# Rope tables in one pass, norms and index scores in PSUM, and the edge of the mixer masks: one change to a two-block model kernel

## The chip, the cores and the metric

The kernel runs as one program on one core of a Trainium2 chip. The metric is the device time of one execution in microseconds (us), taken as the median of several runs. The engines are TensorE (PE, with PEld for its weight loads), VectorE (DVE), ScalarE (ACT), GpSimd (POOL) and SyncE (SP), which here only issues DMAs. Each engine works through its own queue in order.

## What is computed

Two model blocks run one after the other over the same 256 tokens of width 1024, in 32-bit floating point, batch 1. The first block has four layers; layers 0 and 3 use attention over keys chosen by an index score, layers 1 and 2 other attention. Each layer also attends to 256 memory rows, which are normed once, and ends in a gated feed-forward part. Cut to what the change touches:

```python
cos, sin = rope_tables(positions)                  # theta 500000, 8 frequencies
mem_n = layer_norm(mem, mem_ln_g, mem_ln_b)
for i in range(4):
    if i % 3 == 0:
        q, k, v, qi, wi, ki, qm = split_cols(x @ w_in_a[j], ...)
        ki = apply_rope(layer_norm(ki, idx_kn_g[j], idx_kn_b[j]), cos, sin)
        wi = wi * (IDX_HEADS * IDX_DIM) ** -0.5
        # in dsa_attention, for each query block:
        dots = jnp.einsum('bqhd,bsd->bqhs', qi, k_idx)             # 8 heads of 64
        score = jnp.einsum('bqhs,bqh->bqs', jax.nn.relu(dots), wi)
        _, sel = lax.top_k(score, 64)                              # causal; attention to sel alone
    ...
    x = layer_norm(ALPHA * x + mixed, ...); x = layer_norm(ALPHA * x + swiglu(x, ...), ...)
```

The second block has two layers. The first mixes with a recurrence (its decay and causal masks are the "mixer masks") and a gating part, the second with latent attention that has a rope of its own (theta 10000, 16 frequencies, positions 0 to 255). Both attend to a second memory of 256 rows and end in a mixture of 32 experts.

## The kernel before, in words

Tokens lie in two row tiles of 128 (`NT = 2`). A projection (`proj`) streams its weights by SP's DMA in pieces of 1 MB into one of three `raw` buffers; `unit` (L274) splits each 128x512 piece into a high part, written by ACT (L294, `wh`), and a low part, the rest, written by POOL (L296, `wl`), or by DVE in a few stages. `mac` (L304) then issues three products for each piece and row tile (L311 to L313). 12 pairs of weight buffers lie between ACT and POOL on one side and PE on the other. PSUM has three rings: `mm` (4 banks, projection results), `tp` (2 banks, transposes), `at` (2 banks, attention scores). `w2` is a ring of four 128x512 tiles in SBUF for passing values, `sm` a ring of eight small ones.

The program is written in the order of the layers, but each engine's queue is put in order by a planner, which plays the program through with costs of its own and gives an engine the earliest written of the instructions that are ready. An instruction with no late inputs is therefore issued early wherever its engine has a gap in the plan. `issue_after(ins)` adds an edge for order alone to what a block issues: instructions of the block on the engine of `ins` are queued behind `ins`; instructions on other engines get no edge.

What the change and the steps of the prediction touch:

- `setup` (L403) and `setup2` (L914) make the rope tables of the two blocks, for each row tile by itself: an angle, then `rotation` (L423), which calls `sin_reduced` (L449) for cosine and sine (range reduction on DVE, L453 to L464, and a Sin on ACT, L465) and copies each result with a sign (L427, DVE).
- `rotate` (L467) applies a table to a head: three DVE operations (L472 to L474).
- `mem_setup` (L666) norms the two memory tiles on DVE (`norm_affine`: L160 and L166 for halves of 512 columns) and transposes them on PE (L142), with a split by ACT (L150) and DVE (L151).
- `sink_idx` (L739) takes the columns of index weights, index key and memory query out of PSUM. The key norm is L752 to L754 into an SBUF tile `c`, then the rope, then a second copy of the key beside the first (L757), then transposes (L494).
- `topk` (L838) makes the scores: for each group of heads PE writes 512 columns of an `at` bank (L848), ACT copies them through Relu to an SBUF tile (L850), and DVE adds them up, one operation for each head (L853, L855). With row tile 0 there are two groups of four heads with 128 columns each, with row tile 1 four groups of two heads with 256 columns. It is a generator, advanced between the projections of layers 0 and 3.
- `attn_mem` (L635) takes the maximum of memory scores (L655), then Exp on ACT (L659).
- `proj_post` (L199) ends a layer half: the product, a norm of each row tile on DVE (`norm(0)`, `norm(1)`) and the transposes of each (`turn(0)`, `turn(1)`, on PE). It keeps `self.normed`, the last DVE instruction of `norm(1)`. At the join of the two blocks, `mem2_setup` (L976) transposes the second memory and `mixer_masks` (L941, 25 DVE operations and 6 iotas on POOL) makes the masks, both in a block behind `self.normed`. The mask tiles belong to a pool that reuses the SBUF of the first block's pool.

Of the kernel before, what the change touches and what calls it, by code (L numbers as in the profile page):

```python
# [20 lines left out]
NT = 2  # L21
# [13 lines left out]
class K:  # L35
# [163 lines left out]
    def proj_post(self, x, w, kdim, xs, alpha, g, b, xT=None, between=None, **kw):  # L199


        last = []

        def norm(t, ps):
            with self.tc.issue_after(last[-1].ins) if last and not between else nullcontext():
                st = self.ln_stats()
                for i in range(2):
                    self.ln_half(xs[t], ps, alpha, i, st)
                last.append(self.ln_end(xs[t], ps, st, g, b, between=between and (lambda rs: between(t, rs))))

        def turn(t):
            return self.transposed(xs[t], t, xT) if xT else None

        ps = self.proj_full(x, w, kdim, after=lambda ps: norm(0, ps), before=lambda: turn(0), **kw)
        norm(1, ps)
        self.normed = last[-1]
        turn(1)

# [173 lines left out]
D_FF = 2816  # L392
INV_A = [float(np.float32(500000.0) ** np.float32(-np.float32(i) / np.float32(8))) for i in range(8)]
SCALE = 0.125
LAG1 = 8
# [5 lines left out]
class First(K):  # L401

    def setup(self, A):  # L403
        nc = self.nc
        self.A = A
        c = self.const
        self.cmask2 = self.s1.tile([128, 256], F32, name="cmask2")
        nc.vector.tensor_scalar(self.cmask2, self.cmask, NEG, None, op0=OP.add)

        self.cs = c.tile([128, NT, 2, 2, 8], F32, name="cs")  # L410
        inv = c.tile([128, 8], F32, name="inv")
        for i in range(8):
            nc.vector.memset(inv[:, i:i + 1], INV_A[i])
        for t in range(NT):
            pi = self.sm(1, I32)
            nc.gpsimd.dma_start(out=pi, in_=A["positions"][0, t * 128:(t + 1) * 128].rearrange("(p o) -> p o", o=1))
            pf = self.sm(1)
            nc.vector.tensor_copy(out=pf, in_=pi)
            ang = self.sm(8)
            nc.vector.tensor_scalar(ang, inv, pf, None, op0=OP.mult)  # L420
            self.rotation(self.cs[:, t], ang)

    def rotation(self, cs, ang):  # L423

        for j, off in ((0, math.pi / 2), (1, 0.0)):
            self.sin_reduced(cs[:, j, 1, :], ang, off)
            self.nc.vector.tensor_scalar(cs[:, j, 0, :], cs[:, j, 1, :], -1.0 if j else 1.0, None, op0=OP.mult)  # L427

# [19 lines left out]

    def sin_reduced(self, out, ang, off):  # L449
        nc = self.nc  # L450
        n = ang.shape[-1]
        k = self.sm(n)
        nc.vector.tensor_scalar(k, ang, 1.0 / (2 * math.pi), off / (2 * math.pi), op0=OP.mult, op1=OP.add)  # L453
        nc.vector.tensor_scalar(k, k, 12582912.0, 12582912.0, op0=OP.add, op1=OP.subtract)
        r = self.sm(n)
        c1 = 6.28125
# [7 lines left out]
        nc.vector.tensor_scalar(r, r, math.pi, -math.pi, op0=OP.min, op1=OP.max)  # L464
        nc.scalar.activation(out=out, in_=r, func=AF.Sin)  # L465

    def rotate(self, out, h, cs, b):  # L467

        nc = self.nc
        sh = list(h.shape)  # L470
        bc = lambda a: a[:, None].to_broadcast(sh)
        nc.vector.tensor_tensor(b, h[:, :, ::-1, :], bc(cs[:, 1]), op=OP.mult)  # L472
        nc.vector.tensor_tensor(h, h, bc(cs[:, 0]), op=OP.mult)
        nc.vector.tensor_tensor(out, h, b, op=OP.add)  # L474

    def rope(self, out, v, t):
# [3 lines left out]
        b = self.s1.tile([128, 8, 2, 8], F32, tag="rope", name="ropeb", bufs=4)[:, :nh]  # L480
        self.rotate(two(out), two(v), self.cs[:, t], b)

# [183 lines left out]
    def mem_setup(self, ms):  # L666
# [4 lines left out]
        for t, m in enumerate(ms):  # L671
            mv = self.stats(m, D)
            self.norm_affine(m, m, mv, g, b, 1e-5)
            self.transposed(m, t, self.memT)
# [19 lines left out]
    def layer_body(self, i, xs, xT):  # L694
# [40 lines left out]
        if kind == 0:  # L735
# [3 lines left out]
            def sink_idx(chunk, ps):  # L739
                for t in range(NT):  # L740
# [9 lines left out]
                    self.rsqrt(rs, mvv[:, 1:2], 1e-5)  # L750
                    kn = c[:, 0:64]
                    nc.vector.tensor_scalar(kn, kv, mvv[:, 0:1], rs, op0=OP.subtract, op1=OP.mult)  # L752
                    nc.vector.tensor_tensor(kn, kn, kng, op=OP.mult)
                    nc.vector.tensor_tensor(kn, kn, knb, op=OP.add)  # L754
                    self.evac(c[:, 128:384], ps[t][:, 72:328], 256)
                    self.rope(kn[:, None, :], kn[:, None, :], t)
                    nc.vector.tensor_copy(out=c[:, 64:128], in_=kn)  # L757
                    self.qk_transposed(smT, c, t, [0, 128, 256], 4)
# [79 lines left out]
    def topk(self, t, smT, wi, amask):  # L838
# [5 lines left out]
        for hs in [range(a + par, a + 2 * per, 2) for a in range(0, 8, 2 * per) for par in range(2)]:  # L844
            p = self.at((128, per, W))
            for j, h in enumerate(hs):
                r = slice(64 * (h % 2), 64 * (h % 2) + 64)
                nc.tensor.matmul(p[:, j, :], smT[r, h // 2, t * 128:(t + 1) * 128], smT[r, 4, 0:W], start=True, stop=True)  # L848
            rl = self.w2((128, per, W))
            nc.scalar.activation(out=rl, in_=p, func=AF.Relu)  # L850
            for j, h in enumerate(hs):
                if h == 0:
                    nc.vector.tensor_scalar(acc, rl[:, j, :], wi[:, 0:1], 0.0, op0=OP.mult, op1=OP.add)  # L853
                else:
                    nc.vector.scalar_tensor_tensor(acc, rl[:, j, :], wi[:, h:h + 1], acc, op0=OP.mult, op1=OP.add)  # L855
            yield
# [35 lines left out]
DN = 4.0 ** 0.25  # L892
INV_M = [float(np.float32(10000.0) ** np.float32(-np.float32(i) / np.float32(16))) for i in range(16)]
DECAY = -0.5 * math.exp(-0.5)
# [17 lines left out]
class Second(First):  # L912

    def setup2(self, A):  # L914
# [13 lines left out]
        nc.vector.memset(self.ones, 1.0)  # L928

        self.cs2 = c.tile([128, NT, 2, 2, 16], F32, name="cs2")  # L930
        inv = c.tile([128, 16], F32, name="inv2")
        for i in range(16):
            nc.vector.memset(inv[:, i:i + 1], INV_M[i])
        for t in range(NT):
            pos = self.sm(1)
            nc.gpsimd.iota(pos, pattern=[[1, 1]], base=128 * t, channel_multiplier=1, allow_small_or_imprecise_dtypes=True)
            ang = self.sm(16)
            nc.vector.tensor_scalar(ang, inv, pos, None, op0=OP.mult)
            self.rotation(self.cs2[:, t], ang)

# [35 lines left out]
    def mem2_setup(self):  # L976
        nc = self.nc
        self.mem2T = self.pair(self.xa, "mem")
        for t in range(2):
            m = self.raw()[:, 0:D]  # L980
            nc.sync.dma_start(out=m, in_=self.A2["mem"][0, t * 128:(t + 1) * 128, :])
            with self.tc.issue_after(self.normed.ins):
                self.transposed(m, t, self.mem2T, self.at)
# [26 lines left out]
    def mixer_ab(self, xT, side):  # L1010
        nc = self.nc
        A = self.A2
        cols, half = self.params_T()
        with self.tc.issue_after(self.normed.ins):
            self.mixer_masks(self.s2)
# [444 lines left out]
    def rope2(self, out, v, t):  # L1460
        two = lambda x: x.rearrange("p h (a d) -> p h a d", a=2)
        b = self.s2.tile([128, 4, 2, 16], F32, tag="rope", name="ropeb", bufs=4)[:, :v.shape[1]]
        self.rotate(two(out), two(v), self.cs2[:, t], b)

# [545 lines left out]
```

## Time and profile before

| what | value |
|---|---|
| time, median of 3 runs | 2957.38 us (2955.36 to 2957.61) |
| the profiled execution's own time | 2956.99 us |
| its span, first to last instruction | 2954.8 us |
| mean granted TensorE clock | 0.951 of full |
| PE busy | 2623.8 us (89%), 13571 products |
| DVE busy | 1418.1 us (48%), 3091 instructions |
| ACT busy | 897.8 us (30%), 1760 instructions |
| POOL busy | 1024.6 us (35%), 809 instructions |
| moved by DMA | 697.41 MB, mean 236 GB/s |

A row of a timeline is: start in us from the span's start, duration in us, engine, line, operation, tile written and tiles read (names without buffer numbers), shapes, and the count where neighbouring instructions of one kind are merged (the duration is then that of all). In brackets stands how long the engine stood idle before, and what it was waiting for. A row of windows has the stretch, its length, the busy time of PE, PEld, DVE, ACT and POOL with their counts, the granted clock of PE (1.00 is 2.4 GHz, 0.50 is 1.2 GHz), the busy share of DMA and GB/s. A duration holds time in which the instruction had started but could not go on.

### The profile page before, as it was taken

How to read it: one execution, taken by the hardware profiler on the slowest of the kernel's cores; microseconds unless marked ns; L12 is line 12 of the kernel's file. 1: busy time of each engine (PE TensorE's matmuls, PEld its weight loads, DVE VectorE, ACT ScalarE, POOL GpSimd, SP SyncE). 2: the span in 40 equal slices, each digit the busy share in tenths (PEclk: the TensorE clock that was granted, in tenths of full speed). 3: DMA queues.
4: the chain of work that ended last, by engine and by line, in shares of the span. 5: the costliest groups of instructions: out<-in, count | busy, mean ns of one | idle time of the engine just before them, and what ended most of it. 6: DMA issues, size and time to landing. Idle time of an engine off the chain costs nothing. (4 is left out here: it accounts for less than half of the span.)

```text
span 2954.8 us, 36636 instructions
## 1 busy us (share of the span) xinstructions
PE 2623.8 (89%) x13571; PEld 1833.6 (62%) x13571; DVE 1418.1 (48%) x3091; ACT 897.8 (30%) x1760; POOL 1024.6 (35%) x809
## 2 busy tenths in 40 slices
PE   6899999999999998999899989888787899877885
PEld 5678876888778876887788867322232776322331
DVE  8867645765466577675874665110011755100112
ACT  3455443554455445454422132000000642000000
POOL 6445582656645573555444341000000531000000
PEclk8899998999999999999999999999999999999989
DMA  6335552555445543554423346999999547999997
GB/s 199 121 116 188 182 199 86 188 182 191 136 145 187 184 161 115 165 177 162 150 86 103 111 164 234 399 422 421 421 421 401 177 179 280 397 421 421 421 422 307
DMA packets 201220, 697.41 MB, mean 236 GB/s; under 512 B 12874, under 2 KB 43712, under 8 KB 153920
## 3 DMA queue, kind: packets, MB, share of 16 engines
q1 hardware_dynamic: 195264, 676.57, 61.4%
q0 software_dynamic: 5760, 18.32, 1.8%
q8 instruction: 111, 1.82, 0.2%
q14 instruction: 85, 0.70, 0.1%
HBM read 693.80 MB, written 1.05 MB: 235 GB/s over the span
## 5 line engine op out<-in xcount | busy, mean ns | idle before, releaser
L296 POOL TENSOR_TENSOR wl<-raw,wh 128x512 fp32r<-128x512 f32 (+1 forms) x520 | 724.1, 1418 | 604.4 <-ACT wh L294 588.7
L294 ACT ACTIVATE wh<-raw 128x512 fp32r<-128x512 f32 (+1 forms) x776 | 479.7, 628 | 326.5 <-PE mm L312 183.5
L311 PE MATMUL mm<-wh,xh 128*128 128x512 f32 (+2 forms) x1152 | 454.7, 397 | 12.9 <-DVE w L92 8.9
L296 POOL TENSOR_TENSOR wq<-raw,wq 128x512 fp32r<-128x512 f32 (+2 forms) x160 | 206.5, 1315 | 701.8 <-DMA raw<-in_mla_w_in_dram 459.7
L312 PE MATMUL mm<-wh,xl 128*128 128x512 f32 (+2 forms) x1152 | 449.6, 391 | 0.0
L313 PE MATMUL mm<-wl,xh 128*128 128x512 f32 (+2 forms) x1152 | 448.7, 391 | 0.0
L296 DVE TENSOR_TENSOR wl<-raw,wh 128x512 fp32r<-128x512 f32 x256 | 358.9, 1426 | 143.6 <-PE mm L312 90.1
L311 PEld LDWEIGHTS mm<-wh,xh 128*128 128x128 f32 x1152 | 221.2, 192 | 59.8 <-ACT cs L465 9.3
L1877 ACT ACTIVATE w<-at 128x512 f32<-128x512 f32 x16 | 9.6, 597 | 817.9 <-PE at L1869 817.9
L312 PEld LDWEIGHTS mm<-wh,xl 128*128 128x128 f32 x1152 | 221.7, 192 | 43.3 <-issue 1.0
L313 PEld LDWEIGHTS mm<-wl,xh 128*128 128x128 f32 x1152 | 220.4, 191 | 44.2 <-issue 0.7
L294 ACT ACTIVATE wq<-raw 128x512 fp32r<-128x512 f32 (+2 forms) x196 | 109.1, 611 | 247.3 <-issue 117.5
L1665 POOL TENSOR_TENSOR x<-x,gb 128x512 f32<-128x512 f32 x2 | 3.5, 1726 | 465.3 <-DVE x L1664 465.3
L1869 PE MATMUL at<-mraw,xg 128*32 128x512 f32 x432 | 120.2, 678 | 31.6 <-DMA mraw<-in_moe_w_up_dram 22.7
L1869 PE MATMUL at<-wq,xg 128*32 128x512 f32 x464 | 124.2, 662 | 26.3 <-DMA wq<-in_moe_w_up_dram 17.9
L1852 PEld LDWEIGHTS tp<-oh,x 128*128 128x128 f32 x512 | 125.0, 334 | 32.9 <-issue 21.1
L1852 PE MATMUL tp<-oh,x 128*128 128x128 f32 x512 | 130.6, 411 | 14.2 <-PEq L1671 10.1
L1869 PE MATMUL at<-xl,xg 128*32 128x512 f32 x240 | 129.0, 672 | 12.8 <-DMA xl<-in_moe_w_gate_dram 8.5
L1878 DVE SCALAR_TENSOR_TENSOR w<-w,at 128x512 f32<-128x512 f32 x16 | 11.0, 687 | 259.4 <-ACT w L1877 259.4
L311 PE MATMUL mm<-wh,big 128*128 128x512 f32 x352 | 134.4, 391 | 0.0
L312 PE MATMUL mm<-wh,big 128*128 128x512 f32 x352 | 133.2, 389 | 0.0
L1879 DVE SCALAR_TENSOR_TENSOR w<-w,at 128x512 f32<-128x512 f32 x16 | 11.0, 688 | 250.4 <-PE at L1869 250.4
(586 smaller groups left out, 5092.2 us busy)
## 6 DMA issues: line engine op xcount, KB each, us to landing
raw<-in_w_gate_up_dram SPq DMA_DIRECT2D x80, 1024.0 KB, 5.2
raw<-in_w_down_dram SPq DMA_DIRECT2D x44, 1024.0 KB, 4.9
mraw<-in_moe_w_down_dram SPq DMA_DIRECT2D x31, 1024.0 KB, 19.8
wq<-in_moe_w_up_dram SPq DMA_DIRECT2D x30, 1024.0 KB, 19.8
mraw<-in_moe_w_gate_dram SPq DMA_DIRECT2D x28, 1024.0 KB, 19.8
wq<-in_moe_w_gate_dram SPq DMA_DIRECT2D x28, 1024.0 KB, 19.8
raw<-in_moe_w_up_dram SPq DMA_DIRECT2D x26, 1024.0 KB, 19.8
mraw<-in_moe_w_up_dram SPq DMA_DIRECT2D x26, 1024.0 KB, 19.8
```

Of the source, the lines that this page charges most:

```text
L294: nc.scalar.activation(out=hi, in_=src, func=AF.Copy)
L296: (nc.vector if on_dve else nc.gpsimd).tensor_tensor(lo, src, hi.bitcast(F32), op=OP.subtract)
L311: nc.tensor.matmul(p, xh, hi[:, a:b], start=first, stop=False)
L312: nc.tensor.matmul(p, xl, hi[:, a:b], start=False, stop=False)
L313: nc.tensor.matmul(p, xh, lo[:, a:b], start=False, stop=last)
L1665: (nc.vector if t else nc.gpsimd).tensor_tensor(xs[t][:, s], xs[t][:, s], b[:, s], op=OP.add)
L1852: nc.tensor.matmul(p[:, j, :], xs[t].rearrange("p (q k) -> p k q", k=8)[:, kc, :], O[t], start=(t == 0), stop=(t == 1))
L1869: nc.tensor.matmul(p[ss, :], x[:, ss], got[u][m * i + j], start=first, stop=last, tile_position=(0, s0))
L1877: nc.scalar.activation(out=h, in_=gu[0], func=AF.Tanh, scale=0.5)
L1878: nc.vector.scalar_tensor_tensor(h, h, 1.0, gu[0], op0=OP.add, op1=OP.mult)
L1879: nc.vector.scalar_tensor_tensor(h, h, 0.5, gu[1], op0=OP.mult, op1=OP.mult)
```

## The change

One table tile now holds both blocks' frequencies (8 and 16) for both row tiles, made in `setup`, ahead of the first weights in the written order: one range reduction over 48 columns for the cosine and one for the sine, in `w2` tiles, and the signed copies are Sins of their own. `setup2` makes no table. In `sink_idx` the key is normed and scaled in place in its PSUM bank; its columns 16 to 64 and its second copy are written by ACT, the rope reads the bank and writes `c`. In `topk` Relu is done in place in the `at` bank and DVE reads the bank. The memory norm is one ACT operation for each half into an `at` bank, a DVE product in the bank and a DVE sum into SBUF. `self.turned` takes the place of `self.normed`: it is what `turn(1)` returns (`transposed` returns its last PE transpose), or the norm's last instruction where nothing is turned.

```diff
         ps = self.proj_full(x, w, kdim, after=lambda ps: norm(0, ps), before=lambda: turn(0), **kw)
         norm(1, ps)
-        self.normed = last[-1]
-        turn(1)
+        self.turned = turn(1) or last[-1]
...
-        self.cs = c.tile([128, NT, 2, 2, 8], F32, name="cs")
-        inv = c.tile([128, 8], F32, name="inv")
-        for i in range(8):
-            nc.vector.memset(inv[:, i:i + 1], INV_A[i])
+        nf = len(INV_A + INV_M)
+        self.cs = c.tile([128, 2, 2, NT, nf], F32, name="cs")
+        inv = c.tile([128, nf], F32, name="inv")
+        for i, v in enumerate(INV_A + INV_M):
+            nc.vector.memset(inv[:, i:i + 1], v)
+        ang = self.w2()[:, :NT * nf].rearrange("p (t n) -> p t n", t=NT)
+        n1 = len(INV_A)
         for t in range(NT):
             pi = self.sm(1, I32)
             nc.gpsimd.dma_start(out=pi, in_=A["positions"][0, t * 128:(t + 1) * 128].rearrange("(p o) -> p o", o=1))
             pf = self.sm(1)
             nc.vector.tensor_copy(out=pf, in_=pi)
-            ang = self.sm(8)
-            nc.vector.tensor_scalar(ang, inv, pf, None, op0=OP.mult)
-            self.rotation(self.cs[:, t], ang)
-
-    def rotation(self, cs, ang):
-
+            nc.vector.tensor_scalar(ang[:, t, 0:n1], inv[:, 0:n1], pf, None, op0=OP.mult)
+            pos = self.sm(1)
+            nc.gpsimd.iota(pos, pattern=[[1, 1]], base=128 * t, channel_multiplier=1, allow_small_or_imprecise_dtypes=True)
+            nc.vector.tensor_scalar(ang[:, t, n1:nf], inv[:, n1:nf], pos, None, op0=OP.mult)
         for j, off in ((0, math.pi / 2), (1, 0.0)):
-            self.sin_reduced(cs[:, j, 1, :], ang, off)
-            self.nc.vector.tensor_scalar(cs[:, j, 0, :], cs[:, j, 1, :], -1.0 if j else 1.0, None, op0=OP.mult)
+            r = self.reduced(ang, off)
+            for h in range(2):
+                nc.scalar.activation(out=self.cs[:, j, h], in_=r, func=AF.Sin, scale=-1.0 if (j, h) == (1, 0) else 1.0)
...
-    def sin_reduced(self, out, ang, off):
-        nc = self.nc
-        n = ang.shape[-1]
-        k = self.sm(n)
+    def reduced(self, ang, off):
+
+        nc = self.nc
+        like = lambda: self.w2()[:, :NT * ang.shape[-1]].rearrange("p (t n) -> p t n", t=NT)
+        k = like()
...
-        r = self.sm(n)
+        r = like()
...
-        nc.scalar.activation(out=out, in_=r, func=AF.Sin)
+        return r
...
         for t, m in enumerate(ms):
             mv = self.stats(m, D)
-            self.norm_affine(m, m, mv, g, b, 1e-5)
+            rs = self.sm(1, tag="lnrs", bufs=4, pad=4)
+            self.rsqrt(rs, mv[:, 1:2], 1e-5)
+            nm = self.sm(1, tag="lnrs", bufs=4, pad=4)
+            self.nc.vector.tensor_scalar(nm, mv[:, 0:1], rs, -1.0, op0=OP.mult, op1=OP.mult)
+            for i in range(2):
+                s = slice(i * 512, i * 512 + 512)
+                p = self.at()
+                self.nc.scalar.activation(out=p, in_=m[:, s], func=AF.Identity, scale=rs, bias=nm)
+                self.nc.vector.tensor_tensor(p, p, g[:, s], op=OP.mult)
+                self.nc.vector.tensor_tensor(m[:, s], p, b[:, s], op=OP.add)
             self.transposed(m, t, self.memT)
...
-                    kn = c[:, 0:64]
-                    nc.vector.tensor_scalar(kn, kv, mvv[:, 0:1], rs, op0=OP.subtract, op1=OP.mult)
-                    nc.vector.tensor_tensor(kn, kn, kng, op=OP.mult)
-                    nc.vector.tensor_tensor(kn, kn, knb, op=OP.add)
+                    nc.vector.tensor_scalar(kv, kv, mvv[:, 0:1], rs, op0=OP.subtract, op1=OP.mult)
+                    nc.vector.tensor_tensor(kv, kv, kng, op=OP.mult)
+                    nc.vector.tensor_tensor(kv, kv, knb, op=OP.add)
                     self.evac(c[:, 128:384], ps[t][:, 72:328], 256)
-                    self.rope(kn[:, None, :], kn[:, None, :], t)
-                    nc.vector.tensor_copy(out=c[:, 64:128], in_=kn)
+                    self.evac(c[:, 16:64], kv[:, 16:64], 48, on="act")
+                    self.rope(c[:, None, 0:64], kv[:, None, :], t)
+                    self.evac(c[:, 64:128], c[:, 0:64], 64, on="act")
...
-            rl = self.w2((128, per, W))
-            nc.scalar.activation(out=rl, in_=p, func=AF.Relu)
+            nc.scalar.activation(out=p, in_=p, func=AF.Relu)
             for j, h in enumerate(hs):
                 if h == 0:
-                    nc.vector.tensor_scalar(acc, rl[:, j, :], wi[:, 0:1], 0.0, op0=OP.mult, op1=OP.add)
+                    nc.vector.tensor_scalar(acc, p[:, j, :], wi[:, 0:1], 0.0, op0=OP.mult, op1=OP.add)
                 else:
-                    nc.vector.scalar_tensor_tensor(acc, rl[:, j, :], wi[:, h:h + 1], acc, op0=OP.mult, op1=OP.add)
+                    nc.vector.scalar_tensor_tensor(acc, p[:, j, :], wi[:, h:h + 1], acc, op0=OP.mult, op1=OP.add)
...
-            with self.tc.issue_after(self.normed.ins):
+            with self.tc.issue_after(self.turned.ins):
                 self.transposed(m, t, self.mem2T, self.at)
...
-        with self.tc.issue_after(self.normed.ins):
+        with self.tc.issue_after(self.turned.ins):
             self.mixer_masks(self.s2)
```

Left out above: `setup2` loses its table (the loop of `inv`, `pos`, `ang` and `rotation`), and the two callers of `rotate` index the new tile (`self.cs[:, j, :, t, 0:8]` and `8:24`).

## Rows read from the trace of the kernel before

**Rows 1.** Windows: stretch, length, busy PE PEld DVE ACT POOL, clock, DMA

```profile
30.58:98.00 67.42, 45.85 (x203) 37.22 (x203) 64.38 (x180) 19.32 (x40) 38.44 (x34) 0.82 0.51 164
...
35.30:39.90 4.60, 4.59 (x19) 4.60 (x20) 4.53 (x8) 0.00 (x0) 3.40 (x4) 0.50 0.43 137
...
62.25:67.00 4.75, 4.75 (x13) 3.81 (x14) 4.75 (x23) 1.60 (x4) 1.28 (x1) 0.50 0.50 190
...
92.44:98.00 5.56, 5.56 (x18) 4.58 (x18) 4.75 (x20) 0.60 (x1) 0.00 (x0) 0.50 0.07 25
...
98.00:121.60 23.60, 23.51 (x116) 18.06 (x114) 17.49 (x32) 12.17 (x20) 18.80 (x15) 1.00 0.36 119
...
1085.93:1090.60 4.67, 4.67 (x13) 3.81 (x14) 3.96 (x16) 1.54 (x3) 2.13 (x2) 0.50 0.00 0
```

**Rows 2.** Timeline of PE, idle time before rows, layers 0, 3

```profile
35.30 1.94 PE L494 MATMUL tp<-ident,w 128*128 128x128 f32 x8 [4.72 <-DVE w L474]
...
62.25 0.77 PE L311 MATMUL mm<-wh,xh 128*128 128x512 f32 x1 [8.92 <-DVE w L92]
...
81.87 0.66 PE L142 MATMUL tp<-ident,big 128*128 128x128 f32 x4 [2.01 <-DVE big L92]
...
92.44 1.11 PE L142 MATMUL tp<-ident,big 128*128 128x128 f32 x4 [5.23 <-DVE meml L151]
...
1085.93 0.87 PE L494 MATMUL tp<-ident,w 128*128 128x128 f32 x3 [5.39 <-DVE rq L109]
```

**Rows 3.** Timeline of DVE, long operations in layers 0, 3

```profile
17.90 12.87 DVE L427 TENSOR_SCALAR cs<-cs 128x8 f32<-128x8 f32 x1 [0.86 <-ACT cs L465]
...
53.63 6.60 DVE L454 TENSOR_SCALAR sm<-sm 128x16 f32<-128x16 f32 x1
...
75.02 3.50 DVE L166 SCALAR_TENSOR_TENSOR big<-big,lnrs,gb 128x512 f32<-128x512 f32 x2
...
83.25 5.24 DVE L855 SCALAR_TENSOR_TENSOR idx<-w,wi,idx 128x128 f32<-128x128 f32 x1
...
119.89 1.07 DVE L855 SCALAR_TENSOR_TENSOR idx<-w,wi,idx 128x256 f32<-128x256 f32 x1 [0.28 <-ACT w L850]
...
1074.22 10.25 DVE L753 TENSOR_TENSOR w<-w,kn 128x64 f32<-128x64 f32 x1
```

**Rows 4.** Timeline of POOL, three trains of weight splits

```profile
13.25 3.76 POOL L296 TENSOR_TENSOR wl<-raw,wh 128x512 fp32r<-128x512 f32 x3 [8.54 <-ACT wh L294]
...
1065.68 18.71 POOL L296 TENSOR_TENSOR wl<-raw,wh 128x512 fp32r<-128x512 f32 x15
...
1399.60 2.50 POOL L296 TENSOR_TENSOR wq<-raw,wq 128x512 fp32r<-128x512 f32 x2
```

**Rows 5.** Timeline of ACT, first conversions and a table's Sins

```profile
12.54 2.19 ACT L294 ACTIVATE wh<-raw 128x512 fp32r<-128x512 f32 x4 [3.45 <-DMA raw<-in_w_in_a_dram]
...
61.22 0.56 ACT L465 ACTIVATE cs<-sm 128x16 f32<-128x16 f32 x2 [13.05 <-DVE sm L464]
```

**Rows 6.** Timelines of DVE and ACT, rows used as unit costs

```profile
8.05 0.14 DVE L418 CAST sm<-sm 128x1 f32<-128x1 int32 x1
...
9.73 0.16 DVE L453 TENSOR_SCALAR sm<-sm 128x8 f32<-128x8 f32 x1
...
9.93 0.17 DVE L454 TENSOR_SCALAR sm<-sm 128x8 f32<-128x8 f32 x1
...
80.24 0.60 ACT L850 ACTIVATE w<-at 128x512 f32<-128x512 f32 x1 [6.26 <-DVE idx L855]
...
112.83 1.00 DVE L855 SCALAR_TENSOR_TENSOR idx<-w,wi,idx 128x256 f32<-128x256 f32 x2
...
1400.25 1.28 DVE L151 TENSOR_TENSOR meml<-at,memh 128x512 fp32r<-128x512 f32 x2
```

**Rows 7.** Timelines of DVE and PE at the join

```profile
1401.44 2.56 DVE L948 TENSOR_SCALAR rwmask<-w 128x128 f32<-128x128 f32 x2
...
1407.17 0.25 PE L1003 MATMUL tp<-ident,w 38*128 38x38 f32 x1 [2.08 <-DVE xl L151]
```

More of the change, by code (lines that the diff above doesn't have):

```diff
@@ L393 @@
 INV_A = [float(np.float32(500000.0) ** np.float32(-np.float32(i) / np.float32(8))) for i in range(8)]
+INV_M = [float(np.float32(10000.0) ** np.float32(-np.float32(i) / np.float32(16))) for i in range(16)]
 SCALE = 0.125
@@ L471, in rotate @@
         bc = lambda a: a[:, None].to_broadcast(sh)
-        nc.vector.tensor_tensor(b, h[:, :, ::-1, :], bc(cs[:, 1]), op=OP.mult)
-        nc.vector.tensor_tensor(h, h, bc(cs[:, 0]), op=OP.mult)
+        nc.vector.tensor_tensor(b, h[:, :, ::-1, :], bc(cs[1]), op=OP.mult)
+        nc.vector.tensor_tensor(h, h, bc(cs[0]), op=OP.mult)
         nc.vector.tensor_tensor(out, h, b, op=OP.add)
@@ L480, in rope @@
         b = self.s1.tile([128, 8, 2, 8], F32, tag="rope", name="ropeb", bufs=4)[:, :nh]
-        self.rotate(two(out), two(v), self.cs[:, t], b)
+        self.rotate(two(out), two(v), [self.cs[:, j, :, t, 0:8] for j in range(2)], b)
     def big(self, shape, dt=F32):
@@ L892 @@
 DN = 4.0 ** 0.25
-INV_M = [float(np.float32(10000.0) ** np.float32(-np.float32(i) / np.float32(16))) for i in range(16)]
 DECAY = -0.5 * math.exp(-0.5)
@@ L928, in setup2 @@
         nc.vector.memset(self.ones, 1.0)
[L930 to L939, printed above, removed]
     def mixer_masks(self, c):
@@ L1462, in rope2 @@
         b = self.s2.tile([128, 4, 2, 16], F32, tag="rope", name="ropeb", bufs=4)[:, :v.shape[1]]
-        self.rotate(two(out), two(v), self.cs2[:, t], b)
+        self.rotate(two(out), two(v), [self.cs[:, j, :, t, 8:24] for j in range(2)], b)
     def kv_views(self, tiles):
```

## The prediction

> **What bounds the kernel now.** I read the cores first: there is one, so no die to compare, and its mean granted clock is near full. The page's slices then show TensorE (PE) as the busiest engine, with gaps at the very start, at the join of the two blocks and from the experts on, where DMA takes over. The change touches the first layer, the fourth layer (the other one with index scores) and the join of the two blocks, so I went there with the timeline of PE and looked only at rows with idle time in brackets [rows 2]. In layer 0 PE stands for 4.72, 8.92, 2.01 and 5.23 us, 20.88 in all, and in layer 3 for 5.39. After three of these the clock is at its lower level: 4.60, 4.75 and 5.56 us at 0.50 (1.2 GHz), against 1.00 (2.4 GHz) in the stretch behind; after the stop in layer 3 it is 4.67 us at 0.50 [rows 1]. Before each of those PE had been idle for 4.7 us or more; after the idle 2.01 us the clock stayed.
>
> Who made PE wait is in VectorE's (DVE's) rows [rows 3]. The reader is to see durations that the sizes cannot explain: a 128x8 copy of the rope table (L427) for 12.87 us, a 128x16 rounding (L454) for 6.60, an index score (L855) for 5.24, a 128x64 product of the key norm (L753) for 10.25. The last of them shows why: it ends at 1084.47, and a train of 15 GpSimd (POOL) weight splits ends at 1065.68 + 18.71 = 1084.39 [rows 4]. These operations, all between SBUF operands, wait for POOL to run dry. L454's delay also reaches ScalarE (ACT): the Sin of the second block's table stood 13.05 us in ACT's queue [rows 5], with the weight conversions behind it, and that is PE's 8.92.
>
> **Part by part.**
>
> *Tables.* Before: 4 tables (two blocks, two row tiles) of 16 small DVE operations (1 angle, 7 and 6 of range reduction, 2 copies) = 64, and 8 Sins, spread through the opening because the 8-buffer ring of small tiles lets one table through at a time. After: 4 angles, 13 reductions and 4 Sins over 48 columns, and the copies are Sins with scale -1 or 1. The positions are converted at 8.05; at 0.20 us from one dependent operation to the next (9.73 to 9.93) 17 take 3.4 us, two activation splits of 0.64 lie between [rows 6], so they end near 12.7, and POOL's first split starts at 13.25 [rows 4]. Both position loads must therefore go out at once; six small tiles fit the ring, so they can. ACT is idle for 3.45 us before 12.54 [rows 5]; the Sin table load and Sins were there before too. I cost the new pass at nothing, under the wait for the first weights; without that cover it is a rival below. It removes the causes of 4.72 and 8.92 and two of the half-clock stretches.
>
> *Key norm, scores and memory norm in PSUM.* With one operand in PSUM these have at most one SBUF input. Operations of that kind run beside POOL's splits at their plain length: two of L151 (128x512, PSUM and SBUF in) took 1.28 together from 1400.25 on, inside POOL's 1399.60 to 1402.10 [rows 4, 6]. The index score then loses its 5.24 (the cause of PE's 5.23), the memory norm its 3.50 for two halves (the cause of 2.01) [rows 3], the key norm its 10.25 in layer 3 (5.39 of PE). The memory norm costs ACT 4 x 0.60 and DVE 8 x 0.64 instead [rows 6].
>
> *How much comes back.* In layer 0 the stalls and half of the slow stretches make 20.88 + (4.60 + 4.75 + 5.56)/2 = 28.3 us. That is a ceiling: from 30.58 to 98.00 (67.42 us) PE would need 45.85 - 7.46 = 38.4 us at the full clock, but POOL's splits in it also take 38.44 [rows 1]. In the next stretch, where PE never idles, POOL is busy for 18.80 of 23.60, 80%. At that share the stretch takes 48 us and the gain is 19; with both engines packed it is 28. I take **22**, nearer to the neighbouring stretch; the low end is 11 (8.92 and its slow stretch alone). In layer 3 the ceiling is 5.39 + 4.67/2 = 7.7; I take **7** (3 to 7.7), since nothing else there is late. In both layers the memory attention's maximum queues behind two scores of 1.07 and the like that need 0.50 each [rows 3, 6]: **1.5** (0 to 2).
>
> *New waits.* The key's columns 16 to 64 and its second copy go to ACT: 8 copies, each a hop from DVE to ACT and back to PE, queued behind weight conversions (four take 2.19 [rows 5]). Bounds: 0, where ACT is idle, and 4 x 2.4 = 10 where each pair waits for four conversions; the 12 weight buffers cover a wait of a few us, so I take **+1**. No row shows ACT and DVE in one PSUM bank. The Trainium skill (PSUM — Partial Sum Buffer, "PSUM bank collisions raise a hardware error") says that two engines may never touch one bank and quadrant at once, reads included, so that software must order them: by it DVE's rotation of the key waits until ACT's copy out of the same bank is done. By that rule the hop sits inside the DVE chain and the sum would move toward the upper bound, to about 2937; no row here decides it.
>
> *Masks and the second memory.* `turned` is a PE transpose. The block that queues instructions behind it binds only instructions of the same engine, and the masks run on DVE and POOL, so they lose the old edge (a DVE instruction) and get none. The transposes of the second memory do move behind the last turn; they filled a gap in which PE now idles for about a microsecond more, and the products that read them come well after the join. The masks' tiles need the SBUF of the closed pool, so they come free when the last w_down product ends, just as the second row tile's norm starts on DVE. Before, the masks stood between that norm and the last split of xT, two of them taking 2.56 us beside POOL, and PE idled 2.08 [rows 7]. If they go after the split, -2; if they slip into the norm, 13 of them can each lose about 1.28: up to +16, though in the trace most did not wait. I take **+1**, with -2 to +9 for the range.
>
> Sum: -22 - 7 - 1.5 + 1 + 1 = -28.5. The profiled execution took 2956.99 us (span 2954.8 and 2.2 around it), 0.4 under the median of 2957.38, so both stand for one another: **2928.5 us**. What lies behind (layers with PE nearly always busy, then expert stages whose weight loads start when compute frees their buffers) moves up with it.
>
> **Rivals.**
> 1. *Something is late next in layer 0* (POOL's splits, or PE standing in order for transposes whose DVE chain the planner thought shorter): only 11 of the 22 return, 2939.5. For it: POOL and PE need the same 38.4 us. Against: at 98 us the same mix ran with PE at 100%.
> 2. *The tables miss the opening.* If the second position lands late, 17 SBUF-only operations meet POOL's trains, each able to wait up to 12.87, and ACT's Sins block the conversions; that starves POOL and so ends itself, at some 12 us: about 2940. For it: half a microsecond of margin by this count.
> 3. *The change does not do what it says*: the masks are not later but sit inside the norm. +8 on the forecast, 2936.5.
> 4. *Slower*: the two `at` banks. A bank was free after ACT's 0.60; now DVE must finish with it. Memory halves: 0.60 + 2 x 0.64 = 1.88, four of them 7.5. Score groups per layer, at most: 2 x (0.60 + 4 x 0.50) + 4 x (0.60 + 2 x 0.50) = 11.6, two layers 23.2. If PE stands in order for every hold, that is 30.7, two drops of the clock 4.7, and 2.01 + 5.23 + 2.78 do not return: 2928.5 + 45.4 = 2974. It decides from 63% of that price on. Against: with two banks PE works on one while the other drains, and weight products lie between the groups.
>
> **How the numbers follow.** Forecast 0.62 (its own range 2917 to 2937), rival 1 0.17, rival 2 0.07, rival 3 0.08, rival 4 0.06. Low end: all of 28.3 + 7.7 + 2 and no new cost, 2919, with 4 for the masks placed well and a plan that shifts: 2915. The high end takes in rivals 1 to 3 with part of the copies' bound: 2946. Beyond it lie rival 4 and the poor ends of the others. A measurement of this kernel tells about 0.2% (5.9 us) from no change: faster 0.88; same 0.07 (poor ends of rivals 1 and 2, the lower half of rival 4); slower 0.05.
>
> **What would show it.** Right: no DVE operation of layer 0's tables, key norm or scores over 1 us; Sins done by 14 us; no PE idle over 3 us between 20 and 95 us and none near the start of layer 3's attention projections; granted clock 1.00 there. Wrong: PE idle behind `at` banks (rival 4), ACT idle on a DVE reduction (rival 2), masks among the norm's operations with PE waiting at the join (rival 3), or the layer 0 stretch above 55 us with POOL over 80% busy (rival 1).

## The result and the profile after

| kernel | median | range | runs |
|---|---|---|---|
| before | 2957.49 us | 2955.36 to 2958.45 | 4 |
| changed | 2927.61 us | 2926.29 to 2928.92 | 4 |

The ratio is 0.9896, with a 95% interval of 0.9884 to 0.9908: 29.9 us less. The profiled execution of the changed kernel took 2926.29 us, its span is 2924.4. The forecast was 2928.5.

The total was right, and some of the steps that made it up were not. To see where the time came from, I number the 13571 products of PE in the order of issue and compare the start of the same number in both traces. Neighbours can swap places between the kernels, so a single figure is good to a few us. "Again" is a second profile of the changed kernel, taken with later runs (its expectation stands near the end of the experiments).

| stretch (start of product, before) | forecast | gained | again |
|---|---|---|---|
| up to product 40 (21.5 us) | 0 | 1.8 | 0.8 |
| rest of layer 0, to 900 (221 us) | 22 + 0.8 | 22.6 | 22.6 |
| layers 1 and 2, to 4650 (1042 us) | 0 | -1.9 | 1.3 |
| layer 3, to 5400 (1196 us) | 7 + 0.8 | 8.2 | 8.2 |
| join, to 7900 (1660 us) | -1 | 2.0 | -1.2 |
| the rest, to the end of the last | 0 | -3.1 | 0.1 |

(The forecast's 1.5 for the memory attention is halved between the layers; its +1 for the copies on ACT is left out.) Only layers 0 and 3 repeat, and they make 30.8.

First PE, with the idle time and its releaser in brackets, in the opening, in layer 0's attention and in layer 3. These answer to [rows 2].

```profile
38.23 1.09 PE L497 MATMUL tp<-ident,w 128*128 128x128 f32 x4 [5.54 <-DVE bst L122]
...
98.31 1.10 PE L507 MATMUL at<-mkT,big 64*128 64x256 f32 x4 [1.15 <-DVE idx L866]
102.59 2.07 PE L507 MATMUL at<-mkT,big 64*128 64x256 f32 x4 [3.18 <-ACT big L662]
...
1095.24 1.10 PE L507 MATMUL at<-mkT,big 64*128 64x256 f32 x4 [0.52 <-DVE idx L866]
1098.83 3.07 PE L507 MATMUL at<-mkT,big 64*128 64x256 f32 x8 [2.49 <-ACT big L662]
```

And one row of PE in the kernel before, the memory attention of layer 0:

```profile
125.96 2.99 PE L504 MATMUL at<-mkT,big 64*128 64x256 f32 x8 [4.33 <-ACT big L659]
```

Of the five stops the first is left, longer than before (5.54 against 4.72) and later in the order of products (number 112 against 86). The others (8.92, 2.01, 5.23 and layer 3's 5.39) are gone. The stop of the memory attention is still there: 1.15 + 3.18, as much as the one of 4.33 before.

The first stop leads to DVE, POOL and ACT in the opening ([rows 3 to 6] of before):

```profile
4.61 0.19 POOL L424 IOTA sm<- 128x1 f32 x1
4.70 0.60 POOL L419 DMA_DIRECT2D sm<-in_positions_dram  x1
12.00 13.43 POOL L295 TENSOR_TENSOR wl<-raw,wh 128x512 fp32r<-128x512 f32 x12 [6.71 <-ACT wh L293]
25.37 0.15 POOL L424 IOTA sm<- 128x1 f32 x1
25.48 8.43 POOL L295 TENSOR_TENSOR wl<-raw,wh 128x328 fp32r<-128x328 f32 x8
```

```profile
14.59 0.14 DVE L421 CAST sm<-sm 128x1 f32<-128x1 int32 x1
14.77 1.01 DVE L422 TENSOR_SCALAR w<-inv,sm 128x8 f32<-128x8 f32 x1
25.55 8.39 DVE L425 TENSOR_SCALAR w<-inv,sm 128x16 f32<-128x16 f32 x1 [9.77 <-POOL sm L424]
33.98 0.19 DVE L456 TENSOR_SCALAR w<-w 128x48 f32<-128x48 f32 x1
...
36.30 0.19 DVE L467 TENSOR_SCALAR w<-w 128x48 f32<-128x48 f32 x1
```

```profile
29.50 1.28 ACT L429 ACT_TABLE_LOAD   x1
35.59 0.38 ACT L429 ACTIVATE cs<-w 128x48 f32<-128x48 f32 x2 [4.80 <-DVE w L467]
36.52 0.38 ACT L429 ACTIVATE cs<-w 128x48 f32<-128x48 f32 x2 [0.56 <-DVE w L467]
```

The tables missed the opening. The position load of row tile 1 went out at 4.70 but stood behind 1 MB of the memory norm's gain and bias on the same queue: the DMA view gives 9.6 us until it landed, at 14.3, and DVE converts it at 14.59, after POOL's first split at 12.00. (In DVE's queue the conversion also stood behind a split of x that waited for ACT until 13.98, so the load was not the only thing late there.) Worse, the planner queued the second position count behind 12 splits. It came at 25.37, DVE's angle followed at 25.55 and then waited for the next train to end (25.48 + 8.43 = 33.91). The whole reduction, 13 operations, took 2.5 us once POOL was quiet, and the Sins are done at 36.9 instead of 14.

Then windows of the changed kernel (columns as in [rows 1]): 45 us of layer 0 in which PE does about what it did before from 35 to 98, a stretch behind 3.18 us of idle, and 1900 to 2400 by the number of the product, in layer 1.

```profile
28.84:74.20 45.36, 39.82 (x201) 33.18 (x201) 37.74 (x125) 22.86 (x46) 37.28 (x33) 0.96 0.71 237
...
104.00:110.00 6.00, 6.00 (x20) 3.90 (x19) 3.99 (x16) 2.51 (x9) 0.00 (x0) 0.50 0.05 21
...
419.63:530.88 111.25, 106.75 (x501) 81.22 (x500) 64.34 (x185) 48.72 (x100) 44.68 (x34) 0.86 0.36 116
```

Products 86 to 289 took 62.94 us before and 46.20 after, with POOL at 82% of it.

Last the key norm in layer 3, on DVE, and the POOL train in the middle of which it ran. It answers to L753's 10.25 in [rows 3]:

```profile
1049.25 0.35 DVE L763 TENSOR_SCALAR mm<-mm,mv,lnrs 128x64 f32<-128x64 f32 x1
1050.53 0.22 DVE L764 TENSOR_TENSOR mm<-mm,kn 128x64 f32<-128x64 f32 x1
1050.87 0.21 DVE L765 TENSOR_TENSOR mm<-mm,kn 128x64 f32<-128x64 f32 x1
...
1053.97 0.23 DVE L764 TENSOR_TENSOR mm<-mm,kn 128x64 f32<-128x64 f32 x1
```

```profile
1039.59 28.39 POOL L295 TENSOR_TENSOR wl<-raw,wh 128x328 fp32r<-128x328 f32 x24 [4.28 <-ACT wh L293]
```

### The profile page after: what moved, and what is told of

It is laid out like the page before. It is cut to its first block, busy times and chain, and to the rows that moved or that the text cites. A ratio compares the mean times of both kernels' runs of the same rounds, so it can differ in the third digit from the quotient of the medians.

```text
span 2924.4 us, 36619 instructions
## 1 busy us (share of the span) xinstructions
PE 2627.1 (90%) x13571; PEld 1830.2 (63%) x13571; DVE 1367.8 (47%) x3042; ACT 903.0 (31%) x1768; POOL 1021.5 (35%) x809
## 5 line engine op out<-in xcount | busy, mean ns | idle before, releaser
L1868 PE MATMUL at<-mraw,xg 128*32 128x512 f32 x432 | 127.0, 714 | 33.2 <-DMA mraw<-in_moe_w_up_dram 23.7
L1868 PE MATMUL at<-wq,xg 128*32 128x512 f32 x464 | 125.5, 659 | 22.8 <-DMA wq<-in_moe_w_up_dram 17.2
```

Source lines behind the costliest of these rows:

```text
L1868: nc.tensor.matmul(p[ss, :], x[:, ss], got[u][m * i + j], start=first, stop=last, tile_position=(0, s0))
```

## The experiments

The theory: an operation of DVE with SBUF operands only waits while POOL's splits run, one with an operand in PSUM does not; PE's stops in layers 0 and 3 are such waits. Each experiment undoes or does one part. I compare the traces by the numbered products; gains are against the trace of before. Runs that shared a chip: the three with one part alone and the first early table; the three with one part taken back and the first whole table; and the old edge, the changed kernel once more and the whole table once more. Each group had its own runs of the kernel before, and a ratio is against these.

### One part alone

**The tables alone** (the table hunks of the diff on the kernel before).

> The kernel before with the one-pass tables alone. Theory A (the tables caused PE's 8.92 us stop in layer 0, and the parts in PSUM the rest): 8.92 and half of the 4.75 us slow stretch behind it return, 11 to 12 us, so about 2946; the stops of 2.01 and 5.23 us and the one of 5.39 us in layer 3 stay, and so does a stop of about 5 us near 38 us, because the second position count of the table is still queued on POOL behind 12 splits. Rival B (the tables are a small part, the gain is the PSUM part's): within 3 us of before, 2955 or more.

Measured: ratio 0.9965 (0.9953 to 0.9976); the profiled run 2949.44. At product 900 the gain is 9.7. The sum came out near theory A (a median of 2947.87), the rows did not: the stops of 2.01 and 5.23 did not stay as they were. PE and DVE of this kernel:

```profile
56.20 0.52 PE L498 MATMUL tp<-ident,w 128*128 128x128 f32 x3 [1.83 <-DVE w L761]
...
71.32 0.87 PE L498 MATMUL tp<-ident,w 128*128 128x128 f32 x3 [8.40 <-DVE w L761]
```

```profile
57.92 2.99 DVE L758 TENSOR_TENSOR w<-w,kn 128x64 f32<-128x64 f32 x1
...
61.48 7.69 DVE L476 TENSOR_TENSOR ropeb<-w,cs 128x16 f32<-128x16 f32 x1
```

The stop of 8.92 is gone, and one of 8.40 stands in another place: the key norm and the key's rotation, on time now, ran into POOL's splits, where they had come later before. Taking one victim away hands the wait to the next SBUF-only operation in the queue.

**The PSUM parts alone.**

> The kernel before with key norm, index scores and memory norm in PSUM alone, tables and mask edge as before. Theory A: the stops of 2.01 and 5.23 us and half of the 5.56 us slow stretch return (10), layer 3 gives 8 as it did in the changed kernel, the stops of 4.72 and 8.92 us stay: about 2939.5. Rival B (the PSUM part gave nearly all of layer 0's 22.6 us too): about 2927 to 2930. If A holds for both this run and the tables' run, their gains add up to the changed kernel's 29.9 within 3 us.

Measured: ratio 0.9902 (0.9885 to 0.9919), 17.2 at product 900, then 8.9 in layer 3, as theory A has it there. In layer 0 it lies between A and B: with the old tables in place the stop of 8.92 shrank to 2.67 (55.66 us), so not all of it was the table's. The sum of both runs at 900 is 27.0, the changed kernel has 24.4 and 23.4: nearly additive, while the rows that carry the time change places. The medians do not settle it: they gained 10.8 and 26.7 on this chip, 37.5 together, 7.6 more than the 29.9 that the expectation compared with; but the changed kernel itself gained 35.7 on another chip (below).

**The mask edge alone.**

> The kernel before with the mask edge alone. Theory A (the masks go inside the second norm, where POOL has no train of splits, and so cost little; PE's 2.08 us stop at the join goes): 2 to 3 us less, about 2955. Rival B (the masks inside the norm delay it as recorded, up to 1.28 us each): about 2965. Rival C: nothing, 2957.5.

Measured: ratio 1.0009 (0.9999 to 1.0019), by the trace 1.6 less: rival C. And the changed kernel with the old edge:

```diff
-            with self.tc.issue_after(self.turned.ins):
+            with self.tc.issue_after(self.normed.ins):
```

> The changed kernel with the old mask edge, masks queued behind the second norm's last DVE instruction. Theory A (the new edge only moves where PE stands idle at the join, as in the run with the edge alone, where the idle sum between the products 6150 and 7900 was 23.2 us against 22.5 of before): within 1 us in the idle sum of that stretch, the same time within 3 us. Rival B (the edge brought the 2.0 us that the changed kernel gained between 1360 and 1660 us of before): that gain is 0 or negative here, with the same idle sum or more.

Measured: ratio 0.9891 (0.9874 to 0.9907) against 0.9881 (0.9864 to 0.9897) of the changed kernel on the same chip. The medians are 3.9 us apart, 0.9 more than theory A allows; 3.2 of it lie behind product 7900, in the experts, where the first profile of the changed kernel lost as much. From product 6150 to 7900, the idle time of PE in gaps over 0.25 us is 22.5 us before, 24.4 and 24.2 in the two traces of the changed kernel, 23.2 with the edge alone and 25.1 here: within theory A's 1 us. Rival B's sign came as well, since the stretch from 1360 to 1660 us of before gains -1.6 here; but it also gained -1.2 in the second profile of the changed kernel, with the new edge, so that sign does not tell the two apart. The stop of 2.08 at the join [rows 7] is gone with the edge and stands here again (1.74 at 1375.51). In the changed kernel the same time lies elsewhere. PE at the join:

```profile
1360.53 1.29 PE L142 MATMUL tp<-ident,x 128*128 128x128 f32 x8 [1.74 <-DVE x L196]
1366.62 0.50 PE L312 MATMUL mm<-xh 128*128 128x512 f32 x1 [1.24 <-POOL xh L295]
...
1369.57 0.51 PE L312 MATMUL mm<-xl,xh 128*128 128x512 f32 x1 [0.75 <-POOL xl L295]
1370.82 1.28 PE L142 MATMUL tp<-ident,x 128*128 128x128 f32 x8 [0.74 <-DVE x L196]
```

Its 1.74 at the first transposes was 0.86 before. On DVE the masks did slip into the second norm, as rival 3 had it, but at plain length (before, two of L948 took 2.56):

```profile
1363.53 0.36 DVE L947 TENSOR_SCALAR rwmask<-w 128x128 f32<-128x128 f32 x2
...
1363.95 0.28 DVE L964 SCALAR_TENSOR_TENSOR lvm<-w,w 128x128 f32<-128x128 f32 x1
```

### One part taken back

Three versions of the changed kernel with one of the PSUM parts in its old SBUF form, the rest kept. For the key norm:

```diff
-                    nc.vector.tensor_tensor(kv, kv, kng, op=OP.mult)
+                    nc.vector.tensor_tensor(kn, kn, kng, op=OP.mult)
```

> The changed kernel with the key norm back in SBUF tiles, the rest of the change kept. Theory A (the key norm's SBUF operations wait for whole trains of POOL splits, and nothing else covers it): in layer 3 the stop of 5.39 us and its slow stretch return, 8 us as gained there; in layer 0 a stop of 8 us at the key's transposes, as in the kernel with the tables alone. In all about 16 us over the changed kernel, 2943. Rival B (with scores and memory norm in PSUM the key's delay hides behind other products): only layer 3's 8 us, about 2935.

Measured: ratio 0.9911 (0.9894 to 0.9927). At product 900 the gain is 23.4, as with the change whole (24.4 and 23.4); in layer 3 it is 1.3 in place of 8.2. Rival B. DVE, POOL and PE in layer 3:

```profile
1046.74 0.22 DVE L109 TENSOR_SCALAR lnrs<-rq 128x1 f32<-128x1 f32 x1
...
1048.28 10.01 DVE L765 TENSOR_TENSOR w<-w,kn 128x64 f32<-128x64 f32 x1
```

```profile
1039.90 18.30 POOL L295 TENSOR_TENSOR wl<-raw,wh 128x328 fp32r<-128x328 f32 x15
```

```profile
1059.68 0.87 PE L497 MATMUL tp<-ident,w 128*128 128x128 f32 x3 [4.79 <-DVE rq L109]
```

The same product of 128x64 takes 0.22 with one operand in PSUM and 10.01 without, and it ends as POOL's train does (1039.90 + 18.30 = 1058.20). This is the theory in two rows. The row of L109 shows where its wording is too wide: it has SBUF operands only and ran inside the same train in 0.22 us, as did the other one-column operations of the reciprocal root before it. Which operations wait is counted in the last section.

> The changed kernel with Relu and scores back in SBUF tiles, the rest kept. Theory A (the recorded one: the score's wait for POOL caused the stop of 5.23 us in layer 0): DVE has a score of several us again, PE a stop of about 5 us and a slow stretch: 6 to 8 us over the changed kernel, about 2934.5, with 1 to 2 more from the memory attention. Rival B (the key norm was the first cause, and the scores come late only because the key was late): within 3 us of the changed kernel, 2925 to 2931.

Measured: ratio 0.9901 (0.9883 to 0.9918), but the trace is 22.6 at product 900 and 7.9 in layer 3: 0 to 2 us less than with the change whole. That is rival B's time; its cause is not borne out, since the key norm in SBUF cost 0 to 1 us in layer 0 in the run before. The first score in layer 0 takes 0.67 here, in SBUF, and no later one of layer 0 more than 1.30:

```profile
68.13 0.67 DVE L865 TENSOR_SCALAR idx<-w,wi 128x128 f32<-128x128 f32 x1 [1.87 <-ACT w L862]
```

The 5.24 of before [rows 3] was a score that happened to meet a train, and the change of the scores did not take it away. The stop of the memory attention in layer 0 is 5.12 us, 0.8 more than with scores in PSUM.

> The changed kernel with the memory norm back in SBUF tiles, the rest kept. Theory A (recorded): the product with the gain waits for POOL, a stop of PE of about 2 us returns, 2930. Rival B (ACT's four operations and the `at` banks cost as much as the wait): 2926 to 2929. Rival C (the wait is longer than before, since the opening is packed tighter now): a stop of 5 us or more, 2933 or more.

Measured: ratio 0.9917 (0.99 to 0.9934); 15.6 at product 900, which is 7.8 to 8.8 less. By its size this is rival C, but there is no single stop of 5 us: there are two new ones, of 2.04 and 2.84, and behind the second a stretch (63.48 to 69.00) at a granted clock of 0.52. PE and DVE:

```profile
54.78 0.47 PE L310 MATMUL mm<-wh,xh 128*128 128x512 f32 x1 [2.04 <-DVE mm L755]
...
63.48 1.87 PE L851 MATMUL at<-big 64*128 64x128 f32 x11 [2.84 <-DVE big L92]
```

```profile
47.65 2.48 DVE L160 SCALAR_TENSOR_TENSOR big<-big,mv,gb 128x512 f32<-128x512 f32 x2
...
50.51 3.02 DVE L160 SCALAR_TENSOR_TENSOR big<-big,mv,gb 128x512 f32<-128x512 f32 x2
...
57.19 5.32 DVE L166 SCALAR_TENSOR_TENSOR big<-big,lnrs,gb 128x512 f32<-128x512 f32 x2
```

The memory norm's own time has no urgent reader. It holds DVE's queue for 10.8 us in three rows, and the key's norm and the keys' copies stand behind it.

### The table made whole ahead of POOL

First with one position load and one count for both row tiles, ahead of the other loads:

```diff
+        pi = self.sm(NT, I32)
+        nc.gpsimd.dma_start(out=pi, in_=A["positions"][0].rearrange("(t p) -> p t", p=128))
+        pos = self.sm(NT)
+        nc.gpsimd.iota(pos, pattern=[[128, NT]], base=0, channel_multiplier=1, allow_small_or_imprecise_dtypes=True)
```

> The changed kernel with one position load and one position count for both row tiles ahead of the other loads, so that the whole table can be made before the first weights. Theory A (the recorded step was right but for the queue place of the second count): reductions done by 11 us, Sins by 16 us, the 5.54 us stop at 38 us and half of a slow stretch behind it return, about 2920. Rival B (something else is late next there, the head of layer 0 is bound by POOL's splits): under 2 us of it return, 2926 or more. Rival C (the Sins and their table load now delay the first weight conversions): PE starts later by about 2 us and the time is 2928 or more.

Measured: ratio 0.9873 (0.9856 to 0.9889), and a profiled run of 2927.99 with 20.7 at product 900, less than the changed kernel. The stop of 5.54 is gone, a stop of 2.72 is there instead. DVE, then ACT and PE:

```profile
10.84 0.18 DVE L457 TENSOR_SCALAR w<-w 128x48 f32<-128x48 f32 x1
13.94 0.69 DVE L151 TENSOR_TENSOR xl<-tp,xh 128x512 fp32r<-128x512 f32 x1 [2.91 <-ACT xh L150]
14.54 0.51 DVE L464 SCALAR_TENSOR_TENSOR w<-w,w 128x48 f32<-128x48 f32 x1
15.09 1.19 DVE L466 TENSOR_SCALAR w<-w 128x48 f32<-128x48 f32 x1
16.20 1.36 DVE L462 SCALAR_TENSOR_TENSOR w<-w,w 128x48 f32<-128x48 f32 x1
...
21.32 1.16 DVE L467 TENSOR_SCALAR w<-w 128x48 f32<-128x48 f32 x1
```

```profile
22.52 0.38 ACT L429 ACTIVATE cs<-w 128x48 f32<-128x48 f32 x2 [3.10 <-DVE w L467]
```

```profile
23.31 0.64 PE L310 MATMUL mm<-wh,xh 128*128 128x328 f32 x1 [2.72 <-ACT wh L293]
```

The table had a good start and was cut in two: a split of x, queued in its middle, waited 2.91 us for ACT, and the seven operations behind it met POOL at about one split each. The second pair of Sins held ACT, and with it the weights. So theory A's times were missed, and rival C's mechanism (the Sins in the way of the conversions) stands in the trace. Its time does not: the profiled run was the slowest of four, whose median is 2923.99. So the last split of x was queued behind the table's last operation:

```diff
+            with self.tc.issue_after(after.ins) if after is not None and b else ExitStack():
+                self.split(hi[:, 4 * b:4 * b + 4, ts], lo[:, 4 * b:4 * b + 4, ts], p)
```

> The kernel with the early position load and count, and with the last split of x queued on DVE behind the table's last operation. In the run before, that split stood in the middle of the reduction on DVE, waiting for ACT, and the seven operations behind it then met POOL's splits, 1.2 us each. Theory A: the reduction is done by 12.5 us, no DVE operation of it over 0.3 us, the second pair of Sins no longer waits 3.10 us, PE's stop of 2.72 us at 23.31 and half of the slow stretch behind it (5 us at the lower clock) go: 4 to 5 us under the run before in the first 100 us. Rival B (the weights' DMA is late there anyway: the next raw tile lands as late): under 1 us.

Measured: ratio 0.9869 (0.985 to 0.9889), 28.4 at product 900. That is 7.7 more than in the run before, above theory A's 4 to 5; the two ratios, 0.9873 and 0.9869, do not tell the two kernels apart, so what the order edge is worth rests on one trace of the one and two of the other. One operation of the table still met POOL's first split in this run (1.15 us), and the reduction was done at 13.15. The changed kernel and this one once more, on one chip:

> The changed kernel itself, on the chip on which the next two run, so that they are compared with it. All theories: a ratio to the kernel before between 0.988 and 0.991.

> The kernel with the whole table made before POOL's first split, timed beside the changed kernel. Theory A (the 8.8 us by which its trace ended earlier in the run before are the table's): 6 to 9 us under the changed kernel on the same chip, ratio to before 0.986 to 0.988. Rival B (half of it was that run's DMA and clock): 2 to 5 us under it.

Measured: changed 2924.59 (2923.90 to 2925.22), ratio 0.9881 (0.9864 to 0.9897), 35.7 under the kernel before on this chip; whole table 2920.90 (2919.55 to 2922.07), ratio 0.9866 (0.985 to 0.9883). DVE and PE of the last run:

```profile
11.81 0.21 DVE L465 SCALAR_TENSOR_TENSOR w<-w,w 128x48 f32<-128x48 f32 x1
12.05 0.19 DVE L468 TENSOR_SCALAR w<-w 128x48 f32<-128x48 f32 x1
14.39 0.69 DVE L152 TENSOR_TENSOR xl<-tp,xh 128x512 fp32r<-128x512 f32 x1 [2.15 <-ACT xh L151]
```

```profile
46.58 0.47 PE L311 MATMUL mm<-wh,xh 128*128 128x512 f32 x1 [1.86 <-DVE lnrs L109]
```

The reduction is done at 12.24, before POOL's first split of this run (12.92), and the opening has one stop of 1.86 left. At product 900 this is worth 4 to 6 us (28.4 and 29.4 against 24.4 and 23.4), and 3.7 us by the medians, whose ranges do not meet: rival B's size at the end. In the last run's trace 3.2 us were given back between products 2900 and 4400, with a granted clock of 0.97 there against 0.99 in the changed kernel; whether the other executions did so too is not known. This version is the best of all that ran.

## Why the prediction was right, and where it was not

**The bound.** Right: waits of DVE behind POOL's splits, handed on to PE. The 10.01 against 0.22 shows it, and all stops but the first went. Of the signs named for it, three failed, all at the tables: DVE had an operation of 8.39 (and one of 1.01); the Sins were done at 36.9 and not by 14; and PE was idle for 5.54 us at 38 us, with a granted clock of 0.50 from 38.23 to 40.00. The other signs held: no operation of key norm or scores over 1 us, and in layer 3 a clock of 1.00 from 1040 to 1099.

**Tables.** This is the step that failed. "Both position loads must therefore go out at once; six small tiles fit the ring, so they can" counted buffers and left out the queues. The loads did go out early (1.38 and 4.70); what counted was what stands ahead of the load on POOL's DMA queue, and where the planner puts an instruction without inputs among POOL's splits. A cost of nothing was forecast; by the runs with the whole table it costs 4 to 6 us. Rival 2 described it (the second load late, operations behind trains, ACT's Sins blocked), with a chance of 0.07 and a price of 11.5 us.

**Layer 0, -22.** Right in size (22.6 twice) for a reason that mixes two. The choice between 19 and 28.3 was by POOL's share; the stretch then ran at 82% of POOL, close to the 80% read from the neighbour. But the stop of 5.54 and its slow stretch stayed, and without it the stretch takes 41 to 43 us (products 86 to 289, 41.23 and 42.86) in place of 46.2. In those two runs POOL is busy for 92 and 89% of it, so 80% was no limit. The table's miss took about as much as the choice had left in reserve: that the total came within 1 us of the forecast is luck.

**Which part brings what in layer 0.** Wrong by part: the score was given the 5.23 and is worth 0 to 2; the memory norm was given the 2.01 and is worth 7.8 to 8.8; the key norm was given nothing there, and is worth 0 to 1. Each of these is with the other parts in place, so they are not to be added up. Each stop had been put down to the operation that waited in that one trace. The runs show that the waits move to whatever comes next.

**Layer 3, -7.** Right, and half a microsecond over its ceiling of 7.7: 8.2, of which the key norm is 6.9 by the run without it.

**Memory attention, -1.5.** Too much: in layer 0 its stop is 4.33 before and 1.15 + 3.18 after, in layer 3 3.07 before and 0.52 + 2.49 after. The new first parts, 1.15 and 0.52, are waits for an `at` bank that DVE's scores still hold (L866). Against scores in SBUF the gain is 0.8 in layer 0.

**Copies of the key on ACT, +1.** No cost was seen. (The upper bound of 10 is 8.8 by the row of 2.19.) ACT's copy out of the bank ended at 1056.15 and DVE's rotation in the same bank began at 1056.19, after 1.26 us of idle on DVE; no stop of PE is behind it. The Trainium skill (PSUM — Partial Sum Buffer, "PSUM bank collisions raise a hardware error") wants two engines in one bank put in order, and the rows agree: none of the four copies of the key's columns 16 to 64 in the two layers overlaps the rotation. The forecast's step toward 2937 on that account was not needed: at most 1.26 us of DVE's idle time stand behind such a copy.

**Masks, +1.** They went where rival 3 put them, at a price near nothing: POOL had single splits with DMA issues between them there, and the masks of 128x128 took 0.16 to 0.38 each. (The transposes of PE behind the first norm wait 1.74 in place of 0.86, with the edge alone too.) The join gave 2.0 in one trace and -1.2 in the other, so the edge is worth nothing that these runs can tell.

**Rivals 1 and 4.** Neither came in size: the stretch stayed under 55 us. Rival 4's sign did show: PE waits behind `at` banks for 1.15 and 0.52 us, far from the 30.7 of its price.

## What to carry to other kernels

When one engine's operation waits for another engine's train, list every operation that could stand in that place, not the ones that did in one trace: removing single victims can move the wait. With the tables alone a stop of 8.92 went and one of 8.40 came. An operation costed at nothing because it fits ahead of something needs its queue places checked, one by one: the load's queue, the engine's, and what the planner may put in its middle; here, by its one trace, the early start alone gained nothing over the changed kernel at product 900 (20.7), and with an order edge that kept one split out of the middle the traces have 28.4 and 29.4. Compare stretches over two profiles before a difference of 3 us is explained.

## What the runs showed of the hardware

**How long a wait behind POOL lasts.** The Trainium skill (SBUF — State Buffer, "SBUF: two separate sides") says that DVE and POOL share a pair of ports as an exclusive lock, which a DVE operation needs in a two-port mode or with two SBUF inputs, and which is held for one whole instruction. The trace agrees that not every operation of DVE is held up. Among the operations of the changed kernel that began inside one of POOL's splits, the 498 with a tile in PSUM took 0.75 us at most, whatever their size. The 223 scalar operations of one column, all in SBUF, took 0.28 at most. The 335 copies and arithmetic operations on wider tiles, all in SBUF, took 1.36 in the median, about one split. Only one of them, the 8.39, took more than 2 us (in the kernel before there are two, the 12.87 and the 10.25), so a wait for a whole train is the rare case. In the first run with early tables the seven operations waited 0.5 to 1.4 us, each to the end of one split (eight splits took 9.97). In the changed kernel one operation waited 8.39 us through eight splits in a row, and in the run with the key norm in SBUF 10.01. So a lock given back after each instruction explains the one and not the other; why DVE got its turn between the splits there is left open; no run tried it.

**The clock differs where the idle time does not.** After the idle 3.18 us at 102.59 the granted clock was 0.50 for 104 to 110 us. (PE had been idle for 1.15 us a little before, at 98.31.) From product 1900 to 2400, in layer 1, it was 0.91 before, 0.86 after and 0.89 in the second profile, and the stretch took 106.5, 111.3 and 108.1 us, although PE was idle for 6.3 us in the first and 4.5 in the other two. The two profiles of the same kernel differ by 3 us there with the same idle time.

**A small load behind large ones.** The 0.5 KB of positions took 9.6 us to land behind 1 MB on POOL's queue. In the run with early tables 1 KB took 6.5 us as the first one there, while other queues were moving the first weights. In the kernel before, where the load went out at 16.96 with nothing left ahead of it, 0.5 KB took 2.3 us.
